# A two-layer diffusion backbone step: four modulation groups on TensorE, a reordered first call, and early tiles of a third weight group

## The chip, the cores and the metric

The kernel runs on one core of one Trainium2 chip. The metric is the device time of one launch in microseconds (us). TensorE (PE) multiplies matrices, VectorE (DVE) and ScalarE (ACT) work elementwise, and SyncE (SP) issues the loads.

## The reference

One inference step over 128 context tokens and 512 latent tokens, together 640 columns in the kernel. The model has two layers, each of three steps: a SwiGLU, a token mixer (retention and spatial gating in the even layer, differential attention in the odd one) and a second SwiGLU. Every step is modulated by vectors that come from a conditioning vector through a large matrix.

```python
mod = (jax.nn.silu(cond) @ ada_w[i] + ada_b[i]).reshape(-1, N_MOD, D_MODEL)[:, :, None, :]
h = modulate(rms_norm(x, norm_g[i, 0]), mod[:, 0], mod[:, 1])
x = x + 0.5 * mod[:, 2] * swiglu(h, ffn_w_in[i, 0], ffn_w_out[i, 0])
h = modulate(rms_norm(x, norm_g[i, 1]), mod[:, 3], mod[:, 4])
...                                   # out: even_mixer or odd_mixer of h
x = x + mod[:, 5] * out
h = modulate(rms_norm(x, norm_g[i, 2]), mod[:, 6], mod[:, 7])
x = x + 0.5 * mod[:, 8] * swiglu(h, ffn_w_in[i, 1], ffn_w_out[i, 1])
```

with `swiglu(h) = (silu(g) * u) @ w_out`, `[g, u] = h @ w_in`, D_MODEL 1024, D_FF 2816 and N_MOD 9.

## The kernel before

**Phases.** Six phases run one after the other, i = 0 to 5: SwiGLU, even mixer, SwiGLU, SwiGLU, odd mixer, SwiGLU. The activations lie feature by feature with all 640 columns in one row, cut into eight tiles (k = 0 to 7) of 128 features. The columns are worked in two halves of 320 (half 0 and half 1).

**Precision.** Every value is split into a high and a low part. A product takes three matmuls of 128 x 128 by 128 x 320: high weight by high activation (L707), high weight by low activation (L708), low weight by high activation (L709). A weight's high part, `whi`, is a copy on ACT (L320), its low part, `wlo`, a subtraction on DVE (L321). Both have five buffers. `H0p` to `H5p` are the activation tiles of a phase, made by DVE (L619), ACT (L621, high) and DVE (L626, low) in a norm chain, once per half.

**SwiGLU groups.** A SwiGLU has 22 groups of input weights ("fin") in three chunks of 6, 8 and 8, and behind each chunk four groups of output weights ("fout"). The first `NG0` = 3 fin groups of a phase are plain: 2 output columns x 2 halves x 8 k x 3 = 96 matmuls. The others use Strassen's scheme: seven products of 12 matmuls, 84 in all, on sums and differences of activation halves. These sums are the T tiles (DVE L597 to L600 and L521, ACT L594 and L520), built once per phase. The weight sums are four DVE operations (L299 to L302). A Strassen group's products land in PSUM tiles `pu`, `pg`, `pf`, which ACT (L901, L905, L908) and DVE (L912 to L925) evacuate. The first two plain groups of a phase run as a pair: half 0 of both, then half 1 of both. L939 and L940 evacuate them.

**Weight loads.** A list `order` fixes the sequence of all weight groups. SP loads them, 1 MB each, into a ring of two buffers called `raw`. A buffer is free again when its group's last piece has been split, or when a modulation group has been used up. A Strassen group is split in the pieces 0, 1, sums, 2, 3.

**Modulation groups.** There are 36 modulation groups ("ada") for each layer. A group is worked on PE in 16 passes (L459), with two transposes at the end of a set of four, or on DVE in four operations with a reduction (L416 for layer 0, L418 for layer 1). The set `ADV` names those for DVE. The function `weave` places their loads: DVE groups behind fout groups and mixer groups (but not at the places in `skip`), PE groups ahead of chosen fin groups.

**The first call.** The function `first_wide` runs the first pair of phase 0 along a string, `SQ`, of single letters: load modulation groups (`a`, `b`), transposes (`T`), make two H tiles (`F`), fetch the second group and split two pieces of it (`W`), matmuls of group 0 (`G`, both halves) and of group 1 (`g`, half 0). Ahead of it, seven DVE additions (L1547) sum eight tiles of squares, and PE adds up the sum over features by 5 matmuls (L1553, 10 passes in the trace) into `n0p`.

The order on each engine is the order in which this code emits its instructions, after a pass that moves some matmuls.

Of the kernel before, what the change touches and what calls it, by code (L numbers as in the profile page):

```python
# [33 lines left out]
NS = 47  # L34
NG0 = 3
FA = (4, 8, 10, 12, 15, 16, 18, 20)
QD_ = 512
NW = (6, 9)
HP = 60
# [11 lines left out]
LK = 2  # L51
SQ = 'abGTGFabGTGFWaGbGTFggggGGgggg'
NB = (9, 9)
AY = (4, 4)
# [13 lines left out]
def trunk_kernel(  # L68
# [476 lines left out]
    def norm_rstd(i, hf):  # L545
# [171 lines left out]
    def first_wide(i, keys, names):  # L717
# [13 lines left out]
        for c in SQ:  # L731
# [30 lines left out]
        yield ps, 1
        for j in range(2):
# [3 lines left out]
        W1.done()  # L767
        yield ps, 2

    def first_pair(i, keys, names):  # L770
# [6 lines left out]
        for hf in range(2):  # L777
            if hf == 0:
# [43 lines left out]
    def out_proj(keys, acts, l, gmod, nxt, ks=None):  # L822
# [16 lines left out]
        for n_, hf in enumerate((1, 0) if end else (0, 1)):  # L839
            pe_manual((n_ == 1 or keys[0][0] == "fout") and not end)  # L840
            for gi in (2, 3):
# [85 lines left out]
    def ffn(i, l, s, nxt):  # L927
        base = 0
        for ci, n in enumerate(CHUNKS):
# [329 lines left out]
    def odd_mixer(i, nxt):  # L1259
# [256 lines left out]
        for hf in range(2):  # L1516
            pe_manual(hf == 1)
            for gp in range(2):
# [32 lines left out]
    ps = psm("n0p")  # L1551
    for b in range(5):
        PE.matmul(ps[:, b:b + 1], acc[:, b * P:(b + 1) * P], ones[:, 0:1], start=True, stop=True)  # L1553
# [156 lines left out]
```

## Time and profile before

| | us |
|---|---|
| median of 3 runs | 2453.66 (2453.34 to 2454.06) |
| the profiled execution | 2454.91 |
| its span | 2453.1 |

The page gives each engine's busy time over the span. The queries behind it show single instructions: start, duration, engine, line, operation, output and inputs, and, in brackets, the idle time just before it on its engine and what ended it. Tables of stretches give the busy time of each engine and the clock that the throttle granted to PE (1.00 is full speed).

| engine | what it mostly does | busy |
|---|---|---|
| PE | matmuls | 97% |
| DVE | wlo, T tiles, modulation, evacuation | 74% |
| ACT | whi, H tiles, evacuation | 43% |

### The profile page before, as it was taken

The page shows a single profiled execution, that of the slowest core. Times are in us where ns is not written, and L with a number is a line of the kernel's source. Part 1 is how long each engine was busy: PE and PEld are TensorE (multiplying, and loading weights), DVE is VectorE, ACT ScalarE, POOL GpSimd, SP SyncE. Part 2 cuts the span into 40 slices and gives each one's busy share as a digit, 9 for nine tenths or more (in the row PEclk, how much of TensorE's full clock was granted, in tenths as well). Part 3 has the DMA queues.
Part 4 walks back from the last instruction along what each step waited for, and adds up shares of the span by engine and source line. Part 5 has one row for each costly group of instructions (what it writes and reads, how often), then busy time and mean ns, then how long its engine had stood idle before and what let it go on. Part 6 is the DMA issues. An engine that isn't in the chain of part 4 may idle for free.

```text
span 2453.1 us, 40798 instructions
## 1 busy us (share of the span) xinstructions
PE 2391.2 (97%) x16596; PEld 2337.1 (95%) x16596; DVE 1818.8 (74%) x3723; ACT 1065.3 (43%) x2018; POOL 53.0 (2%) x82
## 2 busy tenths in 40 slices
PE   7999999999999999999999999999999999999998
PEld 6899999899999999999999999999999989999998
DVE  7677767877978777667967775779788877574664
ACT  5425345333325344243543423436767645252442
POOL 0000000000000000000000000001011000000000
PEclk9999999999999999999999999999999999999999
DMA  7332423323241423333223342332111112222121
GB/s 270 133 142 86 155 74 114 138 93 131 93 149 52 155 94 134 134 120 138 104 95 120 130 155 104 136 124 75 43 43 58 55 35 74 82 87 87 69 104 43
DMA packets 44476, 259.32 MB, mean 106 GB/s; under 512 B 5888, under 2 KB 8576, under 8 KB 16768
## 3 DMA queue, kind: packets, MB, share of 16 engines
q1 hardware_dynamic: 41024, 252.37, 28.7%
q8 instruction: 130, 2.13, 0.4%
q0 software_dynamic: 1280, 2.62, 0.3%
q10 hardware_dynamic: 1984, 1.72, 0.2%
q14 instruction: 58, 0.48, 0.1%
HBM read 252.76 MB, written 3.93 MB: 105 GB/s over the span
## 4 chain that ended last, share of the span: by engine, by line
PE 80%; DVE 10%; DMA 4%; ACT 3%; issue 1%; POOL 0%; POOLq 0%; ACTq 0%; DVEq 0%
PE op L707 8%; PE op L708 8%; PE op L709 8%; PE pu L707 7%; PE pu L709 6%; PE pu L708 6%; PE pf L707 3%; PE pf L708 3%; PE pg L709 3%; PE pf L709 3%; PE pg L707 3%; PE pg L708 3%; DVE wlo L321 3%; DMA raw<-in_w_fin 3%; ACT whi L320 2%
## 5 line engine op out<-in xcount | busy, mean ns | idle before, releaser
L321 DVE TENSOR_TENSOR wlo<-raw,whi 128x1024 fp32r<-128x1024 f32 (+1 forms) x484 | 534.0, 1119 | 297.9 <-ACT whi L320 295.8
L320 ACT ACTIVATE whi<-raw 128x1024 fp32r<-128x1024 f32 (+2 forms) x483 | 462.4, 975 | 612.2 <-PE op L708 137.9
L818 DVE SCALAR_TENSOR_TENSOR xs<-op,mod,xs 128x128 f32<-128x128 f32 (+2 forms) x312 | 124.2, 434 | 111.9 <-PE op L709 111.6
L416 DVE SCALAR_TENSOR_TENSOR raw<-raw,sb 128x1024 f32<-128x1024 f32 x72 | 87.4, 1219 | 0.6
L536 ACT ACTIVATE nq<-xs 128x320 f32<-128x320 f32 x84 | 38.6, 467 | 112.3 <-DVE xs L818 110.7
L707 PE MATMUL oq<-H4h,whi 128*128 128x320 f32 x256 | 81.1, 318 | 0.2 <-ACT ov L1015 0.2
L709 PE MATMUL oq<-H4h,wlo 128*128 128x320 f32 x256 | 79.6, 311 | 0.0
L708 PE MATMUL oq<-H4l,whi 128*128 128x320 f32 x256 | 79.3, 310 | 0.0
L1352 DVE TENSOR_REDUCE amx<-as 128x1 f32<-128x320 f32 x144 | 61.6, 460 | 19.2 <-PE as L1348 18.8
L418 DVE CUSTOM_DVE_ANT_0 raw<-raw,sb 128x1024 f32<-128x1024 f32 x60 | 72.9, 1220 | 0.7
L1360 ACT ACTIVATE ap<-as,anm 128x320 f32<-128x320 f32 x128 | 66.2, 531 | 14.1 <-DVE anm L1355 13.9
L905 ACT COPY p<-pg 128x320 f32<-128x320 f32 x76 | 32.4, 426 | 57.9 <-PE pg L709 57.8
L708 PE MATMUL pf<-H3p,whi 128*128 128x320 f32 x172 | 54.4, 318 | 1.8 <-DVE H3p L626 1.8
L708 PE MATMUL pf<-H5p,whi 128*128 128x320 f32 x172 | 53.7, 313 | 2.0 <-DVE H5p L626 2.0
L708 PE MATMUL pf<-H2p,whi 128*128 128x320 f32 x172 | 53.5, 313 | 1.8 <-DVE H2p L626 1.8
L707 PE MATMUL pf<-H3p,whi 128*128 128x320 f32 x172 | 54.5, 320 | 0.0
L709 PE MATMUL pf<-H3p,wlo 128*128 128x320 f32 x172 | 54.2, 316 | 0.0
L707 PE MATMUL pf<-H5p,whi 128*128 128x320 f32 x172 | 53.9, 317 | 0.0
L707 PE MATMUL pf<-H2p,whi 128*128 128x320 f32 x172 | 53.8, 316 | 0.0
L707 PE MATMUL pf<-H0p,whi 128*128 128x320 f32 x172 | 53.6, 314 | 0.0
L709 PE MATMUL pf<-H5p,wlo 128*128 128x320 f32 x172 | 53.4, 312 | 0.0
L301 DVE TENSOR_TENSOR raw<-raw 128x512 f32<-128x512 f32 x76 | 52.3, 688 | 1.5
(2691 smaller groups left out, 8805.0 us busy)
## 6 DMA issues: line engine op xcount, KB each, us to landing
raw<-in_w_fin SPq DMA_DIRECT2D x88, 1024.0 KB, 4.7
raw<-in_ada_w SPq DMA_DIRECT2D x64, 1024.0 KB, 4.8
raw<-in_w_fout SPq DMA_DIRECT2D x32, 1024.0 KB, 4.8
raw<-in_w_fout SPq DMA_DIRECT2D x16, 768.0 KB, 4.2
raw<-in_w_oin SPq DMA_DIRECT2D x12, 1024.0 KB, 4.8
raw<-in_w_ein SPq DMA_DIRECT2D x10, 1024.0 KB, 4.8
raw<-in_ada_w SPq DMA_DIRECT2D x32, 256.0 KB, 6.4
raw<-in_w_eout SPq DMA_DIRECT2D x4, 1024.0 KB, 4.9
```

Source lines behind the costliest of these rows:

```text
L301: sub.tensor_tensor(out=a11, in0=a22, in1=a11, op=ALU.subtract)
L320: S.activation(out=hf, in_=t, func=AF.Copy)
L321: sub.tensor_tensor(out=lf, in0=t, in1=hf.bitcast(F32), op=ALU.subtract)
L416: V.scalar_tensor_tensor(out=o, in0=w, scalar=1.0, in1=sb[:, c * D:(c + 1) * D], op0=ALU.mult, op1=ALU.mult, accum_out=r)
L418: V.tensor_tensor_reduce(out=o, in0=w, in1=sb[:, c * D:(c + 1) * D], scale=1.0, scalar=0.0, op0=ALU.mult, op1=ALU.add, accum_out=r)
L536: S.activation(out=q[:, :n], in_=x[k][:, t0:t1], func=AF.Square)
L707: PE.matmul(o, wh, xh, start=start, stop=False, skip_group_check=more)
L708: PE.matmul(o, wh, xl, start=False, stop=False, skip_group_check=more)
L709: PE.matmul(o, wl, xh, start=False, stop=stop, skip_group_check=more)
L818: V.scalar_tensor_tensor(out=x[m][:, a:b], in0=ps[:, a - t0:b - t0], scalar=mod[:, l, gmod * KD + m, c:c + 1], in1=x[m][:, a:b], op0=ALU.m ...
L1352: V.tensor_reduce(out=mx[:, j, a:a + 1], in_=sps[j][a][:, 0:w], axis=AX.X, op=ALU.max, negate=True)
L1360: S.activation(out=pj[j][:, a * 320:a * 320 + w], in_=sps[j][a][:, 0:w], func=AF.Exp, bias=b, accum_out=(sm[:, j, a:a + 1] if full else s2 ...
```

## The change

1. `NG0[0, 0]` is 4: fin group 3 of phase 0 is plain.
2. Modulation groups 20 to 23 of layer 0 leave `ADV`: PE works them, with their loads ahead of fin 7, 8, 9 and 10. In phase 0, nothing is placed behind fout (0,3), (2,2) and (2,3); in phases 2 and 3 nothing behind (0,3) and (2,3). Layer 1's groups are dealt 10 and 10 over phases 2 and 3, where they were 11 and 9.
3. In phases 2, 3 and 5 (`FILL`), 24 matmuls of the third plain group (half 0, k = 0 to 3, both columns) are emitted between the pair's half 0 and half 1.
4. `SQ` is another string with new letters: `h` and `i` run group 0's halves apart, `s` splits one piece, `E` evacuates group 0 and starts the T tiles before group 1's last tiles.
5. `NQ` = 5: DVE sums the first five tiles of squares, and PE adds the other three as well, with a small reduction behind.
6. `NW`, `NB` and `EAD` write the same numbers in another form.

```diff
-NG0 = 3
+NG0 = {(0, 0): 4, (0, 1): 3, (1, 0): 3, (1, 1): 3}
...
-SQ = 'abGTGFabGTGFWaGbGTFggggGGgggg'
+FILL = (2, 3, 5)
+SQ = 'ahbiTGFsabGTGFWaGbGsTFggggGGsEgggg'
+NQ = 5
...
-ADV = {(0, g) for g in range(12, 36)} | {(1, g) for g in range(24) if g // 4 != 2}
+ADV = {(0, g) for g in range(12, 36) if g // 4 != 5} | {(1, g) for g in range(24) if g // 4 != 2}
...
-    order += weave(w00[2:], ada_groups(0, [3, 4, 5]), ada_groups(0, [2]), (2, 3, 4, 5))
+    order += weave(w00[2:], ada_groups(0, [3, 4]), ada_groups(0, [2, 5]), (2, 3, 4, 5, 7, 8, 9, 10), ((0, 3), (2, 2), (2, 3)))
...
-    order += weave(ffn_order(0, 1), l1[:11], pl[:8], FA, ((0, 3),))
-    order += weave(ffn_order(1, 0), l1[11:], pl[8:], FA, ((0, 3),))
+    order += weave(ffn_order(0, 1), l1[:10], pl[:8], FA, ((0, 3), (2, 3)))
+    order += weave(ffn_order(1, 0), l1[10:], pl[8:], FA, ((0, 3), (2, 3)))
...
+            elif c == "E":
+                assert kg == KD
+                yield ps, ((0, 0), (0, 1))
+                W0.done()
+                tb[0] = spawn(tbuild(0))
...
+                if i in FILL:
+                    W = next_group(keys[2])
+                    pa = [psm(f"{names[2]}{j}0") for j in range(2)]
+                    for j in range(2):
+                        for k in range(4):
+                            mm3(pa[j], W, j, k, h[k], 0, k == 0, False)
+                    part[i] = W, pa
...
-        if k:
+        if k >= NQ:
+            qs0.append(q)
+        elif k:
             V.tensor_tensor(out=acc, in0=acc, in1=q, op=ALU.add)
...
-    for b in range(5):
-        PE.matmul(ps[:, b:b + 1], acc[:, b * P:(b + 1) * P], ones[:, 0:1], start=True, stop=True)
+    for n, q in enumerate((*qs0, acc)):
+        for b in range(5):
+            PE.matmul(ps[:, 8 * b + n:8 * b + n + 1], q[:, b * P:(b + 1) * P], ones[:, 0:1], start=True, stop=True)
...
-    V.tensor_scalar(out=m, in0=ps[:, 0:5], scalar1=1.0 / (RS * D), scalar2=EPS / RS, op0=ALU.mult, op1=ALU.add)
+    V.tensor_reduce(out=m, in_=ps[:, 0:40].rearrange("p (b n) -> p b n", n=8)[:, :, 0:KD + 1 - NQ], axis=AX.X, op=ALU.add)
+    V.tensor_scalar(out=m, in0=m, scalar1=1.0 / (RS * D), scalar2=EPS / RS, op0=ALU.mult, op1=ALU.add)
```

Line numbers in the changed kernel are some 8 to 30 higher.

PE's queue at the end of the pair's half 0 in phase 2, in the kernel before. `H2p70` is tile k = 7 of half 0, `H2p01` tile k = 0 of half 1, `whi84`, `whi85` and `whi86` are weights of the first, second and third group, `pf...` PSUM tiles:

```order
L709 MATMUL pf01110_7586<-H2p70_7512,wlo85_1_7685 128x320
L707 MATMUL pf01001_7758<-H2p01_7499,whi84_0_7338 128x320
L708 MATMUL pf01001_7758<-H2p01_7499,whi84_0_7338 128x320
L709 MATMUL pf01001_7758<-H2p01_7499,wlo84_0_7339 128x320
L707 MATMUL pf01011_7759<-H2p01_7499,whi84_0_7338 128x320
```

and the same place in the changed kernel, the first and the last rows of the 24:

```order
L717 MATMUL pf01110_7612<-H2p70_7538,wlo85_1_7711 128x320
L715 MATMUL pf01200_7784<-H2p00_7524,whi86_0_7786 128x320
L716 MATMUL pf01200_7784<-H2p00_7524,whi86_0_7786 128x320
L717 MATMUL pf01200_7784<-H2p00_7524,wlo86_0_7787 128x320
...
L717 MATMUL pf01210_7785<-H2p30_7530,wlo86_0_7787 128x320
L715 MATMUL pf01001_7826<-H2p01_7525,whi84_0_7364 128x320
L716 MATMUL pf01001_7826<-H2p01_7525,whi84_0_7364 128x320
```

The third group's matmuls on half-0 tiles now stand between the last half-0 matmul of the pair and its first half-1 matmul.

SP's queue from the last fout group of phase 0's first chunk on, before (`raw24` is that fout group, `raw26` is fin 6):

```order
L267 DMA raw24_1559<-in_w_fout 128x1536
L264 DMA raw25_1588<-in_ada_w 128x2048
L267 DMA raw26_1658<-in_w_fin 128x2048
L267 DMA raw27_1755<-in_w_fin 128x2048
L267 DMA raw28_1778<-in_w_fin 128x2048
L267 DMA raw29_1863<-in_w_fin 128x2048
```

and changed (`raw25` is fin 6):

```order
L275 DMA raw25_1595<-in_w_fin 128x2048
L272 DMA raw26_1673<-in_ada_w 128x2048
L275 DMA raw27_1757<-in_w_fin 128x2048
L272 DMA raw28_1862<-in_ada_w 128x2048
L275 DMA raw29_1889<-in_w_fin 128x2048
L272 DMA raw30_1998<-in_ada_w 128x2048
L275 DMA raw31_2024<-in_w_fin 128x2048
L272 DMA raw32_2133<-in_ada_w 128x2048
L275 DMA raw33_2159<-in_w_fin 128x2048
L275 DMA raw34_2268<-in_w_fin 128x2048
```

The modulation load ahead of fin 6 is gone, and one stands ahead of each of fin 7 to 10, so that fin and modulation loads alternate between the two buffers.

SP's queue at the end of phase 0, before (`raw54` and `raw56` are the last two fout groups, `in_w_ein` the even mixer's weights):

```order
L264 DMA raw53_4271<-in_ada_w 128x2048
L267 DMA raw54_4469<-in_w_fout 128x2048
L264 DMA raw55_4497<-in_ada_w 128x2048
L267 DMA raw56_4570<-in_w_fout 128x2048
L264 DMA raw57_4601<-in_ada_w 128x2048
L267 DMA raw58_4679<-in_w_ein 128x2048
```

and changed (`raw56` and `raw57` are the last two fout groups):

```order
L275 DMA raw56_4317<-in_w_fout 128x2048
L275 DMA raw57_4508<-in_w_fout 128x2048
L275 DMA raw58_4568<-in_w_ein 128x2048
L275 DMA raw59_4642<-in_w_ein 128x2048
```

The modulation loads ahead of, between and behind the last two fout loads are gone.

More of the change, by code (lines that the diff above doesn't have):

```diff
@@ L34 @@
 NS = 47
-NG0 = 3
+NG0 = {(0, 0): 4, (0, 1): 3, (1, 0): 3, (1, 1): 3}
 FA = (4, 8, 10, 12, 15, 16, 18, 20)
 QD_ = 512
-NW = (6, 9)
+NW = {0: (6, 9)}
 HP = 60
@@ L51 @@
 LK = 2
-SQ = 'abGTGFabGTGFWaGbGTFggggGGgggg'
-NB = (9, 9)
+EAD = {("eout", g): 1 for g in range(4)}
+FILL = (2, 3, 5)
+SQ = 'ahbiTGFsabGTGFWaGbGsTFggggGGsEgggg'
+NQ = 5
+NB = {0: (9, 9)}
 AY = (4, 4)
@@ L198, in trunk_kernel @@
                 wtab["fin", l, s, g] = (w_fin[l * 2 + s, g], KD)
-                if g >= NG0:
+                if g >= NG0[l, s]:
                     stras.add(("fin", l, s, g))
@@ L238, in trunk_kernel @@
     l1, pl = ada_groups(1, (0, 1, 3, 4, 5)), ada_groups(1, (2, 6, 7, 8))
-    order += weave(w00[2:], ada_groups(0, [3, 4, 5]), ada_groups(0, [2]), (2, 3, 4, 5))
-    order += weave([("ein", g) for g in range(10)] + [("eout", g) for g in range(4)], ada_groups(0, [6, 7, 8]))
-    order += weave(ffn_order(0, 1), l1[:11], pl[:8], FA, ((0, 3),))
-    order += weave(ffn_order(1, 0), l1[11:], pl[8:], FA, ((0, 3),))
+    order += weave(w00[2:], ada_groups(0, [3, 4]), ada_groups(0, [2, 5]), (2, 3, 4, 5, 7, 8, 9, 10), ((0, 3), (2, 2), (2, 3)))
+    ads = ada_groups(0, [6, 7, 8])
+    for w in [("ein", g) for g in range(10)] + [("eout", g) for g in range(4)]:
+        order.append(w)
+        for _ in range(EAD.get(w, w[0] == "ein" and w[1] > 1)):
+            order.append(ads.pop(0))
+    assert not ads
+    order += weave(ffn_order(0, 1), l1[:10], pl[:8], FA, ((0, 3), (2, 3)))
+    order += weave(ffn_order(1, 0), l1[10:], pl[8:], FA, ((0, 3), (2, 3)))
     order += [("oin", g) for g in OORD] + [("oout", c, g) for c in range(2) for g in range(2)]
@@ L564, in norm_rstd @@
             V.tensor_scalar(out=dg[:, c0:c1], in0=ident[:, o:P], scalar1=r[:, b:b + 1], scalar2=None, op0=ALU.mult)
-        yield NB[hf]
+        yield NB.get(i, NB[0])[hf]
         bc = psm(name + "b")
@@ L746, in first_wide @@
                 W1 = next_group(keys[1])
+            elif c == "s":
                 split_piece()
-                split_piece()
-            elif c == "G":
+            elif c in "Gh":
                 assert kg < n
-                go(0, kg, W0, (0, 1))
+                go(0, kg, W0, (0, 1) if c == "G" else (0,))
+                kg += c == "G"
+            elif c == "i":
+                go(0, kg, W0, (1,))
                 kg += 1
+            elif c == "E":
[3 more added lines that the diff above has]
+                tb[0] = spawn(tbuild(0))
             elif c == "g":
@@ L758, in first_wide @@
         sg.__exit__(None, None, None)
-        W0.done()
         la[0] = 1
-        yield ps, 0
-        yield ps, 1
+        yield ps, ((1, 0),)
         for j in range(2):
@@ L767, in first_wide @@
         W1.done()
-        yield ps, 2
+        yield ps, ((1, 1),)
+    part = {}
     def first_pair(i, keys, names):
@@ L848, in out_proj @@
                     Ws[gi].done()
-            chains[nxt, hf] = spawn(norm_chain(nxt, hf, NW[hf]))
+            chains[nxt, hf] = spawn(norm_chain(nxt, hf, NW.get(nxt, NW[0])[hf]))
     def op_wide(key, W, acts, l, gmod, nxt):
@@ L947, in ffn @@
                 es = [start_g(0), start_g(1)]
-                for ps, stg in first_pair(i, [("fin", l, s, 0), ("fin", l, s, 1)], [f"pf{l}{s}{a}" for a in range(2)]):
-                    for a in ((0, 1) if stg == 0 else (stg - 1,)):
-                        fin_half(es[a], ps[a, 0, min(stg, 1)], ps[a, 1, min(stg, 1)], min(stg, 1))
+                for ps, stg in first_pair(i, [("fin", l, s, a) for a in range(3)], [f"pf{l}{s}{a}" for a in range(3)]):
+                    for a, hf in (((0, 0), (1, 0)), ((0, 1),), ((1, 1),))[stg] if isinstance(stg, int) else stg:
+                        fin_half(es[a], ps[a, 0, hf], ps[a, 1, hf], hf)
                 acts += [e[:2] for e in es]
                 g0 = 2
-            while g0 < NG0:
+            while g0 < NG0[l, s]:
                 es.append(start_g(g0))
-                W = next_group(("fin", l, s, g0))
+                W, pp_ = part.pop(i, (None, None))
+                W = W or next_group(("fin", l, s, g0))
                 for hf in range(2):
-                    pa = [psm(f"pf{l}{s}{g0}{j}{hf}") for j in range(2)]
+                    late = hf == 0 and pp_ is not None
+                    pa = pp_ if late else [psm(f"pf{l}{s}{g0}{j}{hf}") for j in range(2)]
                     for j in range(2):
-                        mm_fm(pa[j], W, j, hs[i], hf)
+                        for k in range(4 if late else 0, KD):
+                            mm3(pa[j], W, j, k, hs[i][k], hf, k == 0, k == KD - 1)
                     if hf == 1:
@@ L1523, in odd_mixer @@
                     Ws[gp].done()
-            chains[nxt, hf] = spawn(norm_chain(nxt, hf, NW[hf]))
+            chains[nxt, hf] = spawn(norm_chain(nxt, hf, NW.get(nxt, NW[0])[hf]))
     pump()
@@ L1540, in trunk_kernel @@
     acc = stmp("nq0")
+    qs0 = []
     for k in range(KD):
@@ L1593, in trunk_kernel @@
     apply_all2((1,))
-    split_piece()
-    tb[0] = spawn(tbuild(0))
     spe[0] = spawn(splitter())
```

## The prediction

> **What bounds the kernel now.** I read the page's first part, the chain of waits by engine, then how long a load takes from issue to landing, then a table of stretches of the span (width, then busy time of PE, PEld, DVE, ACT and POOL with their counts, the granted PE clock, the DMA share and GB/s).
>
> ```profile
> span 2453.1 us, 40798 instructions
> PE 2391.2 (97%) x16596; PEld 2337.1 (95%) x16596; DVE 1818.8 (74%) x3723; ACT 1065.3 (43%) x2018; POOL 53.0 (2%) x82
> PE 80%; DVE 10%; DMA 4%; ACT 3%; issue 1%; POOL 0%; POOLq 0%; ACTq 0%; DVEq 0%
> ...
> raw<-in_w_fin SPq DMA_DIRECT2D x88, 1024.0 KB, 4.7
> ...
> 100.00:160.00 60.00, 57.75 (x398) 56.18 (x398) 42.04 (x76) 16.92 (x25) 0.00 (x0) 1.00 0.49 176
> 160.00:180.00 20.00, 17.83 (x120) 17.30 (x119) 16.44 (x28) 6.23 (x9) 0.00 (x0) 1.00 0.41 154
> 180.00:260.00 80.00, 80.00 (x548) 80.00 (x547) 62.39 (x93) 42.60 (x65) 0.00 (x0) 1.00 0.23 80
> ...
> 440.00:500.00 60.00, 54.21 (x352) 52.55 (x351) 53.49 (x128) 23.65 (x47) 0.00 (x0) 0.97 0.40 141
> ...
> 740.00:762.00 22.00, 20.22 (x127) 19.80 (x126) 19.83 (x71) 13.85 (x36) 0.00 (x0) 0.92 0.11 45
> ...
> 1180.00:1202.00 22.00, 19.50 (x120) 18.66 (x119) 19.26 (x69) 8.45 (x14) 0.00 (x0) 0.92 0.36 138
> 1202.00:1222.00 20.00, 18.22 (x112) 17.80 (x111) 17.27 (x50) 15.39 (x37) 0.00 (x0) 0.91 0.00 1
> ...
> 2002.00:2024.00 22.00, 19.61 (x120) 18.69 (x119) 20.18 (x72) 13.55 (x33) 0.00 (x0) 0.92 0.06 25
> ```
>
> PE is the bound. So an edit counts by what it does to PE's number of matmuls, to its idle time and to its clock. In the table, a stretch's idle time is its width less PE's busy time, and the work lost to the throttle is the width times one less PEclk. In 740 to 762, that is 1.78 us idle and 22 x 0.08 = 1.76 us of clock. From 180 to 260, PE never stops. In the rows of single instructions below, a note in brackets counts from a matmul's modelled end, so the time lost is 0.16 more. The sum is made against the profiled execution, 2454.91 us (1.8 us outside the span); the median of the runs is 2453.66, 1.25 less.
>
> **The fills (phases 2, 3 and 5).** The same stop stands at three places, here that of phase 2:
>
> ```profile
> 753.00 0.31 PE L709 MATMUL pf<-H2p,wlo 128*128 128x320 f32 x1
> 753.15 0.31 PE L707 MATMUL pf<-H2p,whi 128*128 128x320 f32 x1
> 755.24 0.41 PE L708 MATMUL pf<-H2p,whi 128*128 128x320 f32 x1 [1.78 <-DVE H2p L626]
> 754.84 1.53 DVE L626 SCALAR_TENSOR_TENSOR H2p<-H2t,mod,H2p 128x128 fp32r<-128x128 f32 x5
> 757.08 3.04 DVE L626 SCALAR_TENSOR_TENSOR H2p<-H2t,mod,H2p 128x192 fp32r<-128x192 f32 x10
> 758.00:759.00 1.00, 1.00 (x5) 1.00 (x5) 1.00 (x5) 1.00 (x4) 0.00 (x0) 0.50 0.00 0
> ...
> 779.02 0.82 DVE L521 TENSOR_TENSOR T23bl<-H2t,T23bh 128x640 fp32r<-128x640 f32 x1
> 786.91 0.43 ACT L901 COPY a013s<-pu 128x320 f32<-128x320 f32 x1 [0.49 <-PE pu L709]
> ```
>
> PE starts a matmul each 0.147 us (753.00 to 753.15), waits 2.09 us for the second half's first lo tile, and then runs some 3.4 us at clock 0.50. The change puts 24 matmuls there, 24 x 0.147 = 3.5 us, on first-half tiles that exist. PE then comes to the second half at 756.6, after the first lo tile. From there it takes one k (6 matmuls) in 0.88 us and wants the last at 756.6 + 7 x 0.88 = 762.8; DVE delivers it at 760.1. So nothing is late next in the pair. The next cover is the Strassen tiles: the last T is ready at 779.8, and the first Strassen product now ends at 786.9, so some 3.5 us earlier it still comes after them. Gain per phase: wait and clock, 3.5, 3.6 and 4.1 us in the rows 740, 1202 and 2002; the last holds small stops ahead of the place. I take 3.5 x 3 = **-10.5**. Bounds: -5.8 (the waits alone, 3 x 1.94) and -11.2.
>
> The clock rows decide half of this. [...] The trace shows 0.50 behind a wait of 2.09 us, so the measurement stands.
>
> **Groups 7 to 10 of phase 0.** Four modulation groups go from DVE (L416) to PE (L459), and their loads stand between fin 7, 8, 9 and 10. Phase 2 has such a place already:
>
> ```profile
> 198.64 0.33 SPq L267 DMA_DIRECT2D raw<-in_w_fin  x1
> 210.96 0.33 SPq L267 DMA_DIRECT2D raw<-in_w_fin  x1
> ...
> 1037.10 0.31 PE L709 MATMUL pu<-T23bh,wlo 128*128 128x320 f32 x1
> 1037.34 1.07 PE L459 MATMUL adaps<-raw,sc 128*32 128x256 f32 x16
> 1038.34 0.42 PE L707 MATMUL pu<-H2p,whi 128*128 128x320 f32 x1
> 1038.47 0.33 SPq L264 DMA_DIRECT2D raw<-in_ada_w  x1
> 1040.12 0.33 SPq L267 DMA_DIRECT2D raw<-in_w_fin  x1
> 1046.73 1.58 ACT L320 ACTIVATE whi<-raw 128x1024 fp32r<-128x1024 f32 x2 [2.38 <-DMA raw<-in_w_fin]
> 1049.50 0.41 PE L707 MATMUL pu<-T20bh,whi 128*128 128x320 f32 x1 [0.34 <-DVE p L915]
> 1054.46 2.35 DVE L321 TENSOR_TENSOR wlo<-raw,whi 128x1024 fp32r<-128x1024 f32 x2
> 1055.74 0.41 PE L709 MATMUL pg<-T20ah,wlo 128*128 128x320 f32 x1 [0.88 <-DVE wlo L321]
> ```
>
> One group's passes take 1037.10 to 1038.34, less one pitch: 1.1 us. Four, and two transposes at two pitches: **+4.7**. DVE's 16 operations of 1.22 us (451.60, below) go from here and from the fout chunks, where they count only by the waits named below.
>
> With a modulation load between each two, every fin load goes through the same slot of the two-slot ring: it can start only when the group before has split its last piece. A cycle of that slot, from one wlo_2's end to the next: 1.1 for wlo_3 (the row of two, 1054.46, takes 2.35), a landing, then 8.9 us from landing (1046.73) to wlo_2's end (about 1055.7), in which DVE works its queue in order. The landing is 6.6 us in the row (1040.12 to 1046.73), with the modulation load 1.65 us ahead. When groups wait, the loads draw apart and it comes nearer the page's 4.7. Cycle 14.7 to 16.6, against 12.32 (198.64 to 210.96) + 1.1 = 13.4 of PE work. The first such cycle cost 0.34 + 0.88 + 2 x 0.16 = 1.5 there, its slack used up. Three more can follow, each at 14.7 - 13.4 = 1.3 to 16.6 - 13.4 = 3.2. I take 1.5 and, near the lower end, as the fourth group's load has the other slot again, two at 1.75: **+5.0**. Bounds: +2 (the slack lasts longer) and +11.1 (1.5 + 3 x 3.2). Queued behind a late wlo_0 on DVE stands L915, and PE's last product waits for it, as at 1049.50.
>
> **The end of phase 0.** Two modulation groups behind the last fout groups go.
>
> ```profile
> 451.60 1.22 DVE L416 SCALAR_TENSOR_TENSOR raw<-raw,sb 128x1024 f32<-128x1024 f32 x1
> 451.71 0.33 SPq L267 DMA_DIRECT2D raw<-in_w_fout  x1
> 457.59 0.41 PE L707 MATMUL op<-a0014h,whi 128*128 128x320 f32 x1 [3.13 <-ACT whi L320]
> ```
>
> The fout load was held by a modulation slot until 451.7, and PE waited 3.1 us for it up to 457.59. Now the last two fout loads follow each other. Row 440: 5.8 idle + 60 x 0.03 = 1.8 of clock, 7.6. I take **-6.5**, since a norm chain's wait may stay. Bounds -4.5 and -7.6.
>
> **Smaller waits.** fin 6's tiles stood behind L416 operations on DVE:
>
> ```profile
> 173.39 0.42 PE L707 MATMUL pg<-T00ah,whi 128*128 128x320 f32 x1 [1.47 <-ACT whi L320]
> 174.65 0.42 PE L709 MATMUL pg<-T00ah,wlo 128*128 128x320 f32 x1 [0.70 <-DVE wlo L321]
> ```
>
> One group's 4 x 1.22 = 4.9 us of DVE go ahead of its sums; row 160 has 2.2 idle: **-2.0** (0 to -2.2). Row 100, 2.25 idle before fout 0: the change moves loads a little there, **-0.8** (0 to -2.2). Entry of phase 3, row 1180: 2.5 idle and 1.8 of clock; the last modulation group before it goes, 4.9 us of DVE: **-2.0** (0 to -4.3). That group now stands at phase 3's end: **+0.5** (0 to +2).
>
> **The start.**
>
> ```profile
> 14.63 1.79 PE L1536 MATMUL wu<-zt 128*128 128x128 f32 x8
> 16.26 1.17 PE L1553 MATMUL n0p<-cst,nq 128*128 128x1 f32 x10
> ...
> 68.44 1.93 PE L459 MATMUL adaps<-raw,sc 128*32 128x256 f32 x32 [2.63 <-ACT a000s L939]
> ...
> 92.08 0.41 PE L707 MATMUL pu<-T00ah,whi 128*128 128x320 f32 x1 [0.39 <-ACT a003s L908]
> ```
>
> Three of the DVE additions become passes on PE: 30 more x 0.117 = 3.5 us, and one small reduce on DVE, together some 3.7 (an estimate). DVE's additions weren't what n0p waited for (the warm-up ends at 16.2), so the first tiles come 3.7 later. Against it, DVE has three wlo splits (2.35 for two, above) and two T tiles (0.82, above) fewer ahead of the last tile: 5.1 us. I take nothing for the two together (-1.4 to +3.7). Then PE lost 2.8 us (row 68.44) for evacuations that stood behind T tiles; they now come first: -2.8. The fourth plain group has 96 matmuls for 84: +1.8. The wait at 92.08, 0.55, which now has a plain group ahead of it, goes. Together **-1.6** (-3.0 to +5.5).
>
> NW, NB and EAD spell out values that held before, and move nothing.
>
> **The sum.** -10.5 + 4.7 + 5.0 - 6.5 - 2.0 - 0.8 - 2.0 + 0.5 - 1.6 = -13.2: 2441.7 in the profile, 2440.5 as a median.
>
> **The rivals.**
> - Waits longer than forecast in groups 7 to 10, 11.1 for 5.0: 2446.6. For it: the row's landing of 6.6. Against: the loads draw apart once groups wait.
> - The fills save the waits, and the half clock comes all the same: 10.5 becomes 5.8, 2445. [...] Against: each 0.50 stretch follows its wait.
> - The change doesn't do what it says: the fill itself waits, for the third group's first weights or for two free PSUM banks. It gives nothing, 2451. Against: the third group's matmuls are already pulled forward in the old order, behind the stop.
> - Slower: the one-slot ring gets PE into half clock. If a cycle's whole lack (3.2) falls into one wait, it exceeds the 2.09 us behind which 0.50 was seen, and each costs 3.2 + 1.8 = 5.0. Over groups 7 to 10 and, if the lag isn't worked off, group 11 and fout 0, that is 30 for 5: 2465. It decides from a wait of about 2 us: row 173.39's, 1.47 + 0.31 = 1.78 from start to start, left PEclk at 1.00. Against: the row's lack fell into two places.
>
> **How the numbers follow.** Forecast 0.60, own range 2432 to 2446; long waits 0.15; half clock stays 0.10; fill gives nothing 0.06; slower ring 0.06; better than 2432 0.03. Range 2431 to 2450. 0.2% is 4.9 us, about what a measurement of this kernel can tell from no change. Faster: 0.60 + 0.10 + 0.03 and most of the long waits, 0.84. Same: the rest of these, the empty fill and half the slower ring, 0.11. Slower 0.05.
>
> **What would show it.** In the changed profile: no PE wait above 0.5 us and PEclk 1.00 in the three fill stretches; PE idle for about 5 us over groups 7 to 10 with clock 1.00; no wait of 3 us at the last fout groups; the first H0 tile some 3.7 us later, and no stop of 2.6 us behind the first pair. PEclk below 1.00 in groups 7 to 10, or a new wait ahead of the first Strassen group of phase 2, 3 or 5, would make it wrong.

## The result, and the profile after

| | us |
|---|---|
| before | 2453.62 (2453.34 to 2454.06) |
| after | 2438.92 (2435.57 to 2440.92) |
| after / before | 0.994, 95% interval 0.9923 to 0.9957 |

The change takes 14.7 us off the median, between 10.5 and 18.9 us by the interval. The forecast was 2440.5. The profiled execution of the changed kernel is its fastest, 2435.57 (span 2433.8), and that of the kernel before took 2454.91, so the two traces differ by 19.3 us, 4.6 more than the medians. Among the runs below, one execution (3335 us, at a mean clock of 0.65) is left out of all comparisons.

The first part of the changed kernel's page, and its chain of waits by engine:

```profile
span 2433.8 us, 40951 instructions
PE 2391.9 (98%) x16704; PEld 2337.4 (96%) x16704; DVE 1792.7 (74%) x3682; ACT 1063.4 (44%) x2013; POOL 54.0 (2%) x82
PE 86%; DVE 8%; ACT 3%; DMA 2%; issue 1%; POOL 0%; POOLq 0%; ACTq 0%; DVEq 0%
```

PE is still the bound and has 108 matmul records more than before (16704 for 16596). Its share of the chain rises from 80% to 86%. What went is waiting, for DVE and DMA above all.

The changed kernel's table of stretches, columns as before (width, busy time of PE, PEld, DVE, ACT and POOL, PE's clock, DMA share, GB/s). The places of phases 3 and 5 come 8 and 17 us earlier than before, so their windows are moved:

```profile
100.00:160.00 60.00, 60.00 (x426) 58.81 (x419) 42.57 (x77) 18.03 (x27) 0.00 (x0) 1.00 0.49 183
160.00:180.00 20.00, 20.00 (x138) 20.00 (x137) 12.98 (x21) 6.79 (x10) 0.00 (x0) 1.00 0.22 85
180.00:260.00 80.00, 77.01 (x550) 72.52 (x549) 56.37 (x86) 37.59 (x59) 0.00 (x0) 1.00 0.37 132
440.00:500.00 60.00, 60.00 (x413) 59.84 (x412) 45.72 (x132) 24.60 (x48) 0.00 (x0) 1.00 0.25 88
740.00:762.00 22.00, 22.00 (x150) 21.84 (x150) 19.84 (x70) 16.10 (x38) 0.00 (x0) 1.00 0.00 1
1170.00:1202.00 32.00, 32.00 (x218) 31.68 (x218) 29.37 (x102) 18.71 (x40) 0.00 (x0) 1.00 0.20 67
1990.00:2012.00 22.00, 22.00 (x150) 21.84 (x150) 19.36 (x72) 16.35 (x39) 0.00 (x0) 1.00 0.00 1
```

Every place of this table at which PE stood idle before is full now, at clock 1.00. Only 180 to 260, which was full, now lacks 3.0 us. Both ends of the modulation groups' move can be read here: 7.6 us won in row 440, 3.0 us of waits paid in row 180.

The place at which the paid part stands, in the changed kernel's rows of single instructions (start, duration, engine; the bracket is the idle time before and what ended it):

```profile
197.64 2.35 DVE L329 TENSOR_TENSOR wlo<-raw,whi 128x1024 fp32r<-128x1024 f32 x2
...
198.91 0.42 PE L717 MATMUL pg<-T00ah,wlo 128*128 128x320 f32 x1 [0.80 <-DVE wlo L329]
...
200.02 0.33 SPq L275 DMA_DIRECT2D raw<-in_w_fin  x1
...
212.56 2.35 DVE L329 TENSOR_TENSOR wlo<-raw,whi 128x1024 fp32r<-128x1024 f32 x2
...
213.83 0.41 PE L717 MATMUL pg<-T00ah,wlo 128*128 128x320 f32 x1 [0.88 <-DVE wlo L329]
...
214.94 0.33 SPq L275 DMA_DIRECT2D raw<-in_w_fin  x1
...
229.25 0.42 PE L717 MATMUL pg<-T00ah,wlo 128*128 128x320 f32 x1 [1.21 <-DVE wlo L329]
...
793.65 0.42 PE L717 MATMUL pg<-T20ah,wlo 128*128 128x320 f32 x1 [0.88 <-DVE wlo L329]
```

The last splits of two neighbouring groups (197.64, 212.56) lie 14.9 us apart, and so do their loads (200.02, 214.94): this is the one-slot cycle, and PE waits once in each for the `wlo` of a product that goes to `pg`. The last row is a wait that wasn't there before, one group behind the first Strassen group of phase 2; the same stands in phase 3.

Where the time went, by the start of the first matmul of a kind in the two traces. The fourth column is what was gained or lost since the row above, the fifth what the prediction's terms give for that piece:

| first matmul of | before | after | piece | predicted |
|---|---|---|---|---|
| the first pair (H0) | 26.11 | 28.87 | +2.8 | +3.7 |
| fout 0, phase 0 | 127.76 | 126.62 | -3.9 | -6.1 |
| second chunk's fout | 271.26 | 276.80 | +6.7 | +7.7 |
| even mixer | 634.61 | 631.42 | -8.7 | -6.5 |
| phase 2 | 737.87 | 733.29 | -1.4 | 0 |
| Strassen, phase 2 | 784.89 | 776.73 | -3.6 | -3.5 |
| fout 0, phase 2 | 823.21 | 816.34 | +1.3 | 0 |
| Strassen, phase 3 | 1239.79 | 1224.19 | -8.7 | -5.5 |
| Strassen, phase 5 | 2048.36 | 2027.95 | -4.8 | -3.0 |
| end of span | 2453.1 | 2433.8 | +1.1 | 0 |

Read alone, the table says that nearly every term was right. The experiments say otherwise for the largest, the fills, and for the parts of the start.

### The profile page after: what moved, and what is told of

It reads as the page before. It is cut to its first block, busy times and chain, and to the rows that moved or that the text cites. A ratio compares the mean times of both kernels' runs of the same rounds, so it can differ in the third digit from the quotient of the medians.

```text
span 2433.8 us, 40951 instructions
## 1 busy us (share of the span) xinstructions
PE 2391.9 (98%) x16704; PEld 2337.4 (96%) x16704; DVE 1792.7 (74%) x3682; ACT 1063.4 (44%) x2013; POOL 54.0 (2%) x82
## 4 chain that ended last, share of the span: by engine, by line
PE 86%; DVE 8%; ACT 3%; DMA 2%; issue 1%; POOL 0%; POOLq 0%; ACTq 0%; DVEq 0%
PE op L715 9%; PE op L717 9%; PE op L716 9%; PE pu L715 7%; PE pu L717 6%; PE pu L716 6%; PE pg L717 3%; PE pg L715 3%; PE pg L716 3%; PE pf L715 3%; PE pf L717 3%; PE pf L716 3%; DVE wlo L329 2%; DMA raw<-in_w_fin 1%; PE oq L715 1%; PE atb L1429 1%
## 5 line engine op out<-in xcount | busy, mean ns | idle before, releaser
L424 DVE SCALAR_TENSOR_TENSOR raw<-raw,sb 128x1024 f32<-128x1024 f32 x60 | 72.9, 1220 | 0.6
L1386 ACT ACTIVATE ap<-as,anm 128x320 f32<-128x320 f32 x128 | 66.1, 530 | 14.1 <-DVE anm L1381 13.7
L715 PE MATMUL pf<-H0p,whi 128*128 128x320 f32 x200 | 62.4, 314 | 0.0
L717 PE MATMUL pf<-H0p,wlo 128*128 128x320 f32 x200 | 61.8, 309 | 0.5 <-DVE wlo L329 0.5
L716 PE MATMUL pf<-H0p,whi 128*128 128x320 f32 x200 | 61.6, 309 | 0.0
L715 PE MATMUL pf<-H3p,whi 128*128 128x320 f32 x172 | 53.1, 311 | 0.0
L717 PE MATMUL pf<-H2p,wlo 128*128 128x320 f32 x172 | 53.1, 309 | 0.0
```

What stands on the lines that cost most here:

```text
L424: V.scalar_tensor_tensor(out=o, in0=w, scalar=1.0, in1=sb[:, c * D:(c + 1) * D], op0=ALU.mult, op1=ALU.mult, accum_out=r)
L715: PE.matmul(o, wh, xh, start=start, stop=False, skip_group_check=more)
L716: PE.matmul(o, wh, xl, start=False, stop=False, skip_group_check=more)
L717: PE.matmul(o, wl, xh, start=False, stop=stop, skip_group_check=more)
L1386: S.activation(out=pj[j][:, a * 320:a * 320 + w], in_=sps[j][a][:, 0:w], func=AF.Exp, bias=b, accum_out=(sm[:, j, a:a + 1] if full else s2 ...
```

## The experiments

Seven kernels undo or alter a part of the change, two go on from them, one undoes a part of such a version, and two are the changed kernel again, since an execution's time moves with the clock: on the first chip 21 runs of the kernel before spread from 2447.14 (mean clock 0.993) to 2460.40 (0.988). Ratios are to the kernel before on the same chip, and compared with that of the changed kernel there.

### The changed kernel again

> The changed kernel unaltered, run again. Theory: its runs (2435.6 to 2440.9 so far) differ by how many 3.41-us stretches of half clock they meet: times between 2435 and 2441, and a mean clock lower by 0.001 goes with about 2.4 us more, so the spread is all clock. Rival: loads land sooner or later from run to run, and times differ at one and the same mean clock.

> The changed kernel once more, as the measure for the three runs beside it. Expected 2438 to 2446, mean clock 0.991 to 0.993; of waits of 2 to 3.7 us some are followed by half clock and some not, as the stretches of half clock lie on a grid of 3.41 us that is not tied to the program.

Measured: 2442.36 against 2452.75, ratio 0.9956 (0.9939 to 0.9973); on a second chip 2441.28 against 2453.92, ratio 0.9953 (0.9938 to 0.9967). So the gain is 11 to 12 us there by the ratios, near the lower end of the first interval. The profiled execution of the first repeat took 2442.72, 7.2 us over that of the first result. The stretches at half clock, without the last 15 us of the span, add up to 30.7 us in the former's clock record and 17.1 us in the latter's (34.1 us in the kernel before). At 0.50 half of 13.7, 6.8 us, is lost by the granted clock: by this estimate nearly all of the 7.2 us between these two traces of one kernel is the clock's.

### Without the fills

```diff
-FILL = (2, 3, 5)
+FILL = ()
```

> FILL empty, all else as changed. Theory (a wait of about 2 us and a stretch of half clock come back in each of three phases, 3 x 3.5): 10.5 us above the changed kernel, about 2449, with PEclk 0.50 for 3.4 us behind each of the three waits. Rival (the waits come back without the clock): 5.8 above, about 2445. Rival (later work hid the fills): within 2 us.

Measured: 2446.33, ratio 0.9975 (0.9962 to 0.9987), on the chip of the first repeat: 4.0 us above it by the medians, 4.7 us by the ratios (the means differ by 4.5, with a 95% interval of 1.7 to 7.2). The fills are worth that, not 10.5. The kernel without them has the old stop at its three places:

```profile
740.00:762.00 22.00, 20.22 (x138) 19.80 (x137) 19.83 (x71) 13.57 (x34) 0.00 (x0) 1.00 0.14 49
...
1190.00:1212.00 22.00, 20.22 (x138) 19.80 (x137) 19.83 (x71) 13.79 (x35) 0.00 (x0) 1.00 0.11 45
...
1996.00:2018.00 22.00, 19.62 (x131) 18.71 (x130) 19.79 (x73) 15.16 (x36) 0.00 (x0) 1.00 0.00 1
```

The idle time is that of before (1.78, 1.78, 2.38 us), but the clock is 1.00 in all three rows, where before had 0.92, 0.91 and 0.92. The same wait didn't cost the clock. In the trace of the kernel before, the clock fell to 0.50 at 722.55, 756.68, 1197.00 and 1210.66 us among others, 10, 129 and 4 times 3.413 us apart, so the stretches below are cut at such steps. First the kernel before, the piece with the wait and the next one:

```profile
753.26:756.68 3.42, 1.64 (x12) 1.45 (x11) 3.42 (x12) 3.42 (x11) 0.00 (x0) 1.00 0.00 0
756.68:760.09 3.41, 3.41 (x14) 3.41 (x14) 3.41 (x13) 3.41 (x10) 0.00 (x0) 0.50 0.00 0
```

The same for the kernel without fills, three pieces:

```profile
750.83:754.24 3.41, 3.21 (x22) 2.95 (x21) 3.41 (x13) 3.09 (x10) 0.00 (x0) 1.00 0.01 2
754.24:757.66 3.42, 1.84 (x12) 1.84 (x13) 3.42 (x12) 3.42 (x12) 0.00 (x0) 1.00 0.02 5
757.66:761.07 3.41, 3.41 (x26) 3.41 (x25) 3.41 (x13) 3.41 (x9) 0.00 (x0) 1.00 0.00 0
```

The wait lay wholly inside one piece before, and the next piece ran 14 matmuls in 3.41 us at 0.50. Without the fills the wait is cut in two here (0.20 and 1.58 us), no piece is idle for as long, and the next one runs 26 matmuls at 1.00. That the place of the cut decides is the author's reading of these rows, and was not shown.

Of the 3 x 1.94 = 5.8 us of waiting that the fills do take away, some 2.1 come back: the first fin load behind a modulation load now falls due earlier, and PE waits 1.04 us (0.88 + 0.16, row 793.65 above) in phase 2 and again in phase 3. Without the fills the same stretch has no wait:

```profile
770.00:830.00 60.00, 60.00 (x418) 59.04 (x417) 43.45 (x65) 26.84 (x44) 0.00 (x0) 1.00 0.29 104
```

That leaves 3.7, near the 4.0 to 4.7 measured.

### The modulation groups as before

```diff
-ADV = {(0, g) for g in range(12, 36) if g // 4 != 5} | ...
+ADV = {(0, g) for g in range(12, 36)} | ...
-    order += weave(w00[2:], ada_groups(0, [3, 4]), ada_groups(0, [2, 5]), (2, 3, 4, 5, 7, 8, 9, 10), ((0, 3), (2, 2), (2, 3)))
+    order += weave(w00[2:], ada_groups(0, [3, 4, 5]), ada_groups(0, [2]), (2, 3, 4, 5))
```

> Modulation groups 20 to 23 of layer 0 back on DVE and phase 0's loads in the old places; fills, start and the plain fourth group stay. Theory (4.7 of passes and 3.9 of waits go, 7.6 at the end of phase 0 and 2.2 at fin 6 come back, by the rows of both profiles): 1 to 2 us above the changed kernel, about 2440.5. Rival (the end of phase 0 is worth nothing by itself, the fourth plain group or the start cured it): 8 below, 2431. Rival (DVE's load is the cost): 10 above, 2449.

Measured: 2442.81, ratio 0.9960 (0.9944 to 0.9977), 0.45 us above the first repeat on that chip, which can't be told from nothing (the means differ by 1.3 us, give or take 3.6). Its row at the end of phase 0 is that of the kernel before, 5.6 us idle and 0.97:

```profile
440.00:500.00 60.00, 54.44 (x356) 53.03 (x355) 53.69 (x135) 23.59 (x47) 0.00 (x0) 0.97 0.40 141
```

So the four groups on PE, as placed, win nothing: the passes and the waits at fin 7 to 10 eat up what the end of phase 0 gives.

### Modulation loads further apart

```diff
...
-(2, 3, 4, 5, 7, 8, 9, 10)
+(2, 3, 4, 5, 8, 11, 15, 18)
...
```

Three fin loads or more now stand between two of the four modulation loads, so that the fin loads have both slots of the ring again.

> The loads of the four modulation groups on PE stand ahead of fin 8, 11, 15 and 18, not 7 to 10. Theory (the one-slot cycle of 14.9 us against 13.4 of PE work makes the waits): with plain fin loads between them the waits of 1.1, 1.2 and 1.5 us in groups 8 to 10 go, some 3.7 us less than the changed kernel, about 2435, and the spread between runs shrinks. Rival (each modulation group on PE brings its wait wherever it stands): same as the changed kernel, 2439.

Measured: 2437.44, ratio 0.9938 (0.9921 to 0.9955), 4.9 us below the first repeat by the medians (the means differ by 4.4, with an interval of 0.8 to 7.9). The row of the waits is full:

```profile
180.00:260.00 80.00, 79.99 (x560) 78.01 (x560) 60.07 (x89) 40.58 (x63) 0.00 (x0) 1.00 0.29 106
```

So the alternating loads were the cause, and the three waits that they brought (0.80, 0.88 and 1.21 from the modelled ends, 0.16 more each) were 3.4 us.

### The same in phases 2 and 3

`FA` lists the fin groups of phases 2 and 3 ahead of which a modulation group for PE is loaded. This kernel also has the spaced loads of the one before.

```diff
-FA = (4, 8, 10, 12, 15, 16, 18, 20)
+FA = (6, 8, 10, 12, 14, 16, 18, 20)
```

> Modulation groups on PE spaced out everywhere: phase 0 ahead of fin 8, 11, 15, 18; phases 2 and 3 ahead of fin 6, 8, 10, 12, 14, 16, 18, 20 (4, 8, 10, 12, 15, 16, 18, 20 in the changed kernel). Theory (a modulation load between two neighbouring fin loads brings a wait of 1.1 to 1.2 us; fin 4's in phases 2 and 3 gave back part of the fills): the waits near 790, 1047, 1240 and 1495 go too, 4.2 us, with 3.7 from phase 0 some 8 us below the changed kernel. Rival (the wait near 790 and 1240 comes from the fill itself, as it brings PE there earlier than DVE's sums): those two stay, 6 below.

Measured: 2432.22, ratio 0.9916 (0.9902 to 0.9931), 9.1 us below the second repeat. Row 180 stays full, and so are now both places of the wait in phases 2 and 3:

```profile
180.00:260.00 80.00, 79.87 (x558) 77.67 (x557) 58.82 (x88) 39.15 (x63) 0.00 (x0) 1.00 0.29 107
770.00:830.00 60.00, 60.00 (x411) 60.00 (x411) 46.90 (x73) 26.22 (x42) 0.00 (x0) 1.00 0.23 81
1220.00:1260.00 40.00, 40.00 (x275) 40.00 (x274) 30.32 (x44) 19.96 (x32) 0.00 (x0) 1.00 0.24 81
```

### The fills, where nothing is given back

The kernel before this one, with `FILL = ()`.

> fa6 with FILL empty. In the changed kernel taking the fills away cost 4.3 us by the medians, where the prediction had 10.5. Theory (each fill saves a wait of 1.94 us in any case, 5.8 in three phases; half clock behind it comes only when most of the wait lies in one stretch of the 3.41-us grid; and two waits near 790 and 1240, 1.04 each, that only the fills brought, gave 2.1 back): without those two, the fills are worth 5.8 and a part of 5.1 of clock, so 6 to 9 above fa6's 2432, at 2438 to 2441. Rival (the fills are worth about 4 for another reason, nothing is given back): 2436.

Measured: 2440.25, ratio 0.9933 (0.9921 to 0.9946), on a third chip. Against the ratio of the version with fills that is 0.17%, 4.2 us, against its median 8.0 us; the two ran on different chips, and the size stays open between them. Here the wait in phase 2 was followed by half clock, again cut at steps of 3.41 us:

```profile
747.20:750.62 3.42, 1.64 (x11) 1.38 (x10) 3.42 (x13) 3.15 (x11) 0.00 (x0) 1.00 0.00 0
750.62:754.03 3.41, 3.41 (x15) 3.41 (x14) 3.41 (x12) 3.41 (x10) 0.00 (x0) 0.50 0.02 5
```

and the one in phase 5 was not:

```profile
2003.31:2006.72 3.41, 1.64 (x12) 1.38 (x11) 3.41 (x13) 3.38 (x9) 0.00 (x0) 1.00 0.00 0
2006.72:2010.13 3.41, 3.41 (x23) 3.41 (x24) 3.41 (x12) 3.41 (x11) 0.00 (x0) 1.00 0.02 5
```

For the same three waits half clock followed at three of three places in the kernel before (0.50 from 756.68, 1210.66 and 2019.62 on) and at none of three without the fills (1.00 in all three rows); here it followed in phase 2 and not in phase 5. The last two rows don't fit the reading by the place of the cut: this wait too lies inside one piece, PE is busy for the same 1.64 us, and the clock stays at 1.00.

### The squares summed on DVE again

```diff
-NQ = 5
+NQ = 8
```

> NQ = 8: DVE sums all eight tiles of squares, PE adds 5 matmuls as in the kernel before; the string of the first call stays. Theory (30 passes more on PE delay the first tiles, nothing waited for DVE): first H0 matmul about 2.7 to 3.7 us earlier than in the changed kernel (28.9 there, 26.1 before), and no second stretch of half clock near 20 us, since PE's one-column matmuls count as idle: 2 to 5 us less in all. Rival (later loads and modulation groups set the start): the first tiles come earlier and the first Strassen product starts within 0.5 us of where it did.

Measured: 2436.55, ratio 0.9933 (0.9917 to 0.9949), 4.7 us below the second repeat by the medians; with five and four runs the interval reaches from nothing to 9.3. The prediction had set the cost of `NQ` against DVE's fewer operations. The changed kernel's start, single rows, and the stretch behind:

```profile
14.47 1.20 PE L1562 MATMUL wu<-zt 128*128 128x128 f32 x8
15.51 6.26 PE L1583 MATMUL n0p<-cst,nq 128*128 128x1 f32 x40
...
28.87 0.41 PE L715 MATMUL pf<-H0p,whi 128*128 128x320 f32 x1
```

```profile
14.59:18.00 3.41, 3.41 (x32) 3.41 (x32) 0.00 (x0) 0.37 (x1) 0.00 (x0) 1.00 0.99 357
18.00:24.83 6.83, 6.83 (x41) 5.54 (x41) 2.69 (x16) 1.14 (x2) 0.00 (x0) 0.50 1.01 365
```

And the same rows with `NQ` = 8, then its stretch:

```profile
16.54 1.33 PE L1583 MATMUL n0p<-cst,nq 128*128 128x1 f32 x10
...
23.94 0.41 PE L715 MATMUL pf<-H0p,whi 128*128 128x320 f32 x1
```

```profile
16.87:23.70 6.83, 6.72 (x67) 5.22 (x67) 4.49 (x23) 2.73 (x5) 0.00 (x0) 1.00 1.03 391
```

The 40 one-column passes take 6.3 us and not the 4.7 that 40 x 0.117 would make. The piece from 18.00 on is at half clock, though PE was busy in all of the piece ahead of it. The first H0 matmul comes at 28.87 with them, at 23.94 without. The other traces bear this out: the first fout group starts at 126.6, 128.9 and 129.8 us in the three traces of the changed kernel, at 123.0 with `NQ` = 8 here and in the last version below.

### Three plain groups in phase 0

```diff
-NG0 = {(0, 0): 4, (0, 1): 3, (1, 0): 3, (1, 1): 3}
+NG0 = {(0, 0): 3, (0, 1): 3, (1, 0): 3, (1, 1): 3}
```

> NG0[0, 0] = 3: fin group 3 of phase 0 is a Strassen group again. Theory (12 matmuls for a plain group, and time for the T tiles): 1.8 us of matmuls less, but the first Strassen product now meets T tiles that are built late, a wait of over 2 us ahead of it: within 2 us of the changed kernel. Rival (the T tiles are ready anyway): 1.8 us below.

Measured: 2449.56, ratio 0.9977 (0.9967 to 0.9988), 8.3 us above the second repeat, though PE has 12 matmuls less to do. The early Strassen groups, single rows and a stretch:

```profile
103.50 0.42 PE L715 MATMUL pg<-T00ah,whi 128*128 128x320 f32 x1 [0.63 <-ACT whi L328]
104.82 0.41 PE L717 MATMUL pg<-T00ah,wlo 128*128 128x320 f32 x1 [0.76 <-DVE wlo L329]
```

```profile
80.00:130.00 50.00, 46.48 (x334) 42.82 (x333) 33.14 (x50) 23.73 (x37) 0.00 (x0) 1.00 0.43 154
```

A plain group needs no weight sums and no T tiles. It costs 1.8 us of PE, and without it PE waits 3.5 us here for `whi` and `wlo`; in the changed kernel the row from 60 to 130 is full (shown below). That it gives DVE and ACT the time to get ahead fits these rows, but it isn't the whole 8.3. The profiled execution is 7.0 us behind that of the second repeat, 2.1 us at the first fout group and 3.1 at the end of phase 0. Most of what follows is lost in the even mixer, at a wait that the second repeat doesn't have:

```profile
678.02 1.02 PE L1049 MATMUL ot3a<-cst,on 128*128 128x128 f32 x4 [2.08 <-DVE on L1067]
```

Why a group of phase 0 brings that wait stays open.

### T tiles at the old place, with the new string

The T tiles are started ahead of the first pair again, and no longer by `E`.

```diff
-                tb[0] = spawn(tbuild(0))
...
+    tb[0] = spawn(tbuild(0))
```

> The building of T tiles starts ahead of the first call, as in the kernel before, not behind group 0's evacuation; all else as changed. Theory (the evacuation of the first pair stood behind T tiles on DVE and ACT): a PE wait of 2 to 3 us comes back behind the first pair, near 68, and the total is some 2.5 above the changed kernel. Rival (the new string alone keeps the evacuation in front): no such wait, same time.

Measured: one time that can be used, the profiled one, 2456.38. The start, single row and stretch:

```profile
78.04 0.64 PE L715 MATMUL pf<-H0p,whi 128*128 128x320 f32 x1 [5.11 <-ACT whi L328]
```

```profile
0.00:60.00 60.00, 47.14 (x312) 36.83 (x312) 31.10 (x88) 23.48 (x46) 0.21 (x4) 0.81 0.66 241
```

PE stands 5.1 us for a `whi` that ACT makes behind T tiles, and the first Strassen group comes 15 to 18 us later than in the three traces of the changed kernel. The time itself is 12 to 17 us above that kernel: 12 if its ratio of 0.9953 on the second chip is carried over to this one (1.0004 here), 17 against the first median. It is one execution on a chip on which the changed kernel did not run, so the size is rough.

### The whole start as before

`SQ`, `NQ`, `NG0` and the place of the T tiles and of the evacuations together, as in the kernel before; the rest changed.

```diff
-NG0 = {(0, 0): 4, (0, 1): 3, (1, 0): 3, (1, 1): 3}
+NG0 = {(0, 0): 3, (0, 1): 3, (1, 0): 3, (1, 1): 3}
...
-SQ = 'ahbiTGFsabGTGFWaGbGsTFggggGGsEgggg'
-NQ = 5
+SQ = 'abGTGFabGTGFWaGbGTFggggGGgggg'
+NQ = 8
...
```

> The whole start of the kernel before (its string, NQ = 8, three plain groups in phase 0, T tiles from the beginning); modulation groups, their places and the fills as changed. Alone, NQ = 8 took 4.7 us off the changed kernel, a Strassen group 3 added 8.3, and T tiles from the beginning 15 to 18. Theory (these parts fit one another: the old string needs the early T tiles for its early Strassen group, and the parts of the start cancel, as the profiles of both kernels have the first fout group at 127.8 and 126.6): 1 to 3 us above the changed kernel, a ratio to the kernel before of 0.996 to 0.997. Rival (the single effects add up): some 18 above, slower than the kernel before.

Measured: 2443.01 against 2452.44, ratio 0.9957 (0.9943 to 0.9972), on the chip of the first repeat with 0.9956. The new start, which holds the title's "reordered first call", makes no difference that can be measured (the means differ by 0.1 us, give or take 3.3). In the traces, the old start in this kernel:

```profile
0.00:60.00 60.00, 48.02 (x363) 38.11 (x364) 45.24 (x117) 30.75 (x59) 0.21 (x4) 0.94 0.75 276
60.00:130.00 70.00, 64.86 (x472) 61.32 (x472) 45.49 (x72) 34.00 (x56) 0.00 (x0) 1.00 0.34 128
```

and the changed kernel:

```profile
0.00:60.00 60.00, 50.13 (x370) 40.86 (x371) 36.93 (x107) 25.34 (x51) 0.21 (x4) 0.91 0.68 242
60.00:130.00 70.00, 70.00 (x512) 66.89 (x511) 44.76 (x69) 36.23 (x57) 0.00 (x0) 1.00 0.42 157
```

The new start wins 5.1 us of idle time from 60 to 130 and 2.1 up to 60, but loses clock there (60 x 0.03 = 1.8 us) and has more passes to do.

### A version from these parts

The spaced loads, `FA` as above, and `NQ` = 8, all else as changed.

> The changed kernel with two edits from the runs before: the loads of modulation groups on PE spaced out (as in fa6) and NQ = 8 (as in nq8). Theory (the two savings lie at different places, 9 and 4.7 us by their medians): some 13.5 us below the changed kernel, about 2428, and 25 us below the kernel before. Rival (both only gave the start or groups 7 to 10 the slack that the other takes): no more than 9 below, 2432.

Measured: 2424.57 against 2455.46, ratio 0.9876 (0.9863 to 0.9889), some 30 us below the kernel before. Its interval lies wholly below that of every other version here.

```profile
span 2421.8 us, 40902 instructions
PE 2386.9 (99%) x16674; PEld 2334.3 (96%) x16674; DVE 1794.6 (74%) x3685; ACT 1062.4 (44%) x2013; POOL 54.2 (2%) x82
```

## Why the prediction was right, and where it was wrong

The total was right, in direction and size: 2440.5 forecast, 2438.92 measured, 2442.36 and 2441.28 on the other chips. But several terms were wrong and offset one another, so that it came so near is in part luck.

- **The fills, -10.5: the step that failed.** The prediction reasoned "each 0.50 stretch follows its wait" and counted a lost 1.7 us of clock into each of the three. The places were right, PE no longer stops there, and nothing is late next in the pair. But the same wait, 1.78 us from the modelled end, was followed by 0.50 at three of three places in the kernel before and at none of three without the fills, and in the version with the loads spaced and no fills in phase 2 (0.50) but not in phase 5 (1.00). What is sure are the waits, 5.8, and the two new waits give back 2.1: 3.7, with 4.0 to 4.7 measured. The rival that the half clock stays had the size nearly right, for another reason: in the trace without the fills no half clock came (1.00 in its three rows). The prediction took three rows that agreed with one another for a rule, and they were rows of one execution.
- **"Nothing is late next"** held for the pair and the first Strassen group, which the prediction named. One group further, behind a modulation load, PE waited for `wlo`, 1.04 us each in phases 2 and 3.
- **Groups 7 to 10.** The one-slot cycle was forecast with 14.7 to 16.6 us and came with 14.9. The waits were 3.4 us for a forecast of 5.0. The forecast set the cycle against 13.4 us of PE work, but PE worked 13.9 us in it (14.92 less the wait of 1.04), and the first of the cycles lacked 0.96 where 1.5 was taken. The spaced loads show the cause. The longest wait was 1.37 us (1.21 + 0.16), and the clock stayed at 1.00 (row 180): neither the long waits nor the slower rival came. That half clock "decides from a wait of about 2 us" isn't borne out by the kernel before: from start to start, a wait of 1.87 us (1194.13 to 1196.00) was followed by 0.50 from 1197.00 on, and one of 2.94 us (65.50 to 68.44) by 1.00.
- **The end of phase 0, -6.5.** Row 440 gave its whole 7.6, and the piece up to the even mixer 8.7 in the trace. Passes, waits, fin 6 and this end sum to +1.2 by the forecast (4.7 + 5.0 - 6.5 - 2.0), and to -0.45, give or take some 3.6, by the kernel with the old modulation groups: nearly nothing, as forecast.
- **Entry of phase 3, -2.0.** The row from 1170 is full at 1.00, so the 4.3 of the old row 1180 went, the upper bound. The traces without the fills, with the old modulation groups and with the old start have no stop there either (1170 to 1202: PE busy for 32.00 us in each), so the gain is none of theirs. That leaves the other dealing of layer 1's groups, which no run undid alone.
- **The start, -1.6.** The sum holds (no difference measured), its parts do not. `NQ` was set off to nothing and costs 4.7 by the medians. The fourth plain group was booked with its +1.8 of matmuls and is worth 8.3 the other way. The parts can't be added: with the late T tiles undone alone the kernel loses some 12 to 17 us (one execution), with the whole start undone nothing.
- **The chances.** Those for same and slower, 0.11 and 0.05, aren't what their parts add up to: the rest of the long waits (0.04), the empty fill (0.06) and half the slower ring (0.03) are 0.13, which leaves 0.03. Nothing else rests on it.
- **What stays open.** Undone one at a time, the fills (4.0), the modulation groups (0.45) and the start (0.6) sum to 5.1 of the 10.4 us between the medians on that chip. The entry of phase 3 can hold up to 4.3 of the rest. How much the fills are worth when nothing is given back, 4 or 8 us, stays open too.

## What to carry to other kernels

Here a stall's idle time was the same in the kernel before and without the fills (1.78, 1.78 and 2.4 us), and the throttled stretch behind it was not (the rows' clocks are 0.92, 0.91 and 0.92 against 1.00). Book the first, and keep the second for the range, unless several executions show it. The length of a wait alone didn't tell, in one trace of the kernel before: with waits of 3.13 us (up to 457.59), 3.57 us (up to 723.22) and 1.55 us (up to 1196.00) the clock fell to 0.50 at 459.73, 722.55 and 1197.00, and with one of 2.63 us (up to 68.44) it stayed at 1.00. Where loads of two kinds share a short ring, don't let them alternate: with three fin loads between two modulation loads nothing was lost here, and some 4 to 5 us were won. Parts of a reordered start that look like plain costs, a dearer group above all, may save more than they cost elsewhere, so try each part alone before it is dropped or kept.

## What the hardware showed unasked

In the trace of the kernel before, the clock fell to 0.50 nine times, at 9.16, 459.73, 722.55, 756.68, 1197.00, 1210.66, 1988.90, 2019.62 and 2442.87 us. From one to the next these are 132, 77, 10, 129, 4, 228, 9 and 124 times 3.413 us. In the changed kernel's it fell at 11.17, 18.00, 721.14, 1970.42 and 2420.98 us, 2, 206, 366 and 132 times 3.413 us apart. PE's idle time in the 3.41 us ahead doesn't order these falls from the rest: in the kernel before it was 1.35 us from 1985.48 on, with 0.50 in the next 3.41 us, and 1.85 us from 452.90 on, with 1.00 in the next.

Half clock also came behind a stretch that the profile has as busy throughout. In the changed kernel, 14.59 to 18.00, with warm-up matmuls and a part of the 40 passes with one column, has PE busy for 3.41 of 3.41 us, and from 18.00 to 24.83 the clock was 0.50. With 10 such passes it was 1.00 from 16.87 to 23.70 (`NQ` = 8) and from 16.00 to 459.72 (the kernel before).
